# Norm factors from transposes, bursts moved off instruction borders, and a few reordered splits in a retention and HGRN2 step

## The chip, the cores and the metric

The kernel runs on one core of one Trainium2 chip. Its time is the device time of one execution in microseconds (us). Five engines run side by side, each with its own instruction stream: TensorE (PE in the profile; PEld are its weight loads), VectorE (DVE), ScalarE (ACT), GpSimd (POOL) and SyncE (SP), which issues most transfers.

## The reference

One layer of a decoder step. The input is normalised, projected to eight groups of 512 columns, and two kinds of heads run on them: four retention heads (rotary, fixed decay) and four HGRN2 heads (a forget gate per element). Both are normalised per head, gated, concatenated and projected back. 2048 prompt tokens run from a zero state, and 8 single tokens from given states.

```python
def rmsnorm(x, g):
    return x * lax.rsqrt(jnp.mean(x * x, axis=-1, keepdims=True) + NORM_EPS) * g

def mixer_layer(x, pos, s_ret, s_hg, norm_g, w_in, ret_g, hg_g, lb, w_out):   # cut
    h = rmsnorm(x, norm_g)
    p = (h @ w_in).astype(jnp.float32)            # 1024 -> 8 x 512
    rq, rk, rv, rg, hq, hf, hi, hgate = jnp.split(p, 8, axis=-1)
    rq, rk = rotary(rq, pos), rotary(rk, pos) * RET_DK ** -0.5
    o_ret, s_ret_new = chunked_decay_recurrence(rq, rk, rv, log_gamma, s_ret)
    o_ret = head_rmsnorm(o_ret, ret_g) * jax.nn.silu(rg)
    logf = jnp.logaddexp(jnp.log(lb), jnp.log1p(-lb) + jax.nn.log_sigmoid(hf))
    kin = (1.0 - lb) * jax.nn.sigmoid(-hf)
    o_hg, s_hg_new = chunked_decay_recurrence(jax.nn.silu(hq), kin, hi, logf, s_hg)
    o_hg = head_rmsnorm(o_hg, hg_g) * jax.nn.silu(hgate)
    return x + jnp.concatenate([o_ret, o_hg], -1) @ w_out, s_ret_new, s_hg_new
```

The outputs are the final-normalised results of prompt and sample and the four new states.

## The kernel before

**Products in three parts.** Every large fp32 product is made of three: each operand is split into a high and a low part (`hi_lo`: ACT rounds, DVE subtracts), and `three` runs high x high, high x low, low x high in a reduced fp32 form in which a matmul is one record of the profile. A plain fp32 matmul is two records; a transpose is one. Each record has a weight load beside it.

**Stage 1, the token pairs (to about 580 us).** The tokens are 8 pairs of 256. For each pair and each of three sets of weight columns, a seven-product scheme (`CHAIN`: operands `A..`, `S1` to `S4` of the tokens, `B..`, `T1` to `T4` of the weights) gives the projections for values, gates, queries and keys in banks `pv<pair><a to d>`. `v_pair(i, after)` writes one pair in program order; the lists `after[n]` say what is emitted behind product n of it: loads, splits, sums of the next weights, and the small matmuls `pgd` for the sample tokens (`wg_decode`, whose weights `wgr` are loaded by `wg_load` and stored as `ws..T` sums by `wg_spool`). The first set normalises the tokens: `rs_all` holds the factor of each token in a column, one per 128 tokens, computed on POOL. A product needs it along the free axis in every partition. `spread_dg` makes diagonal matrices on DVE (identity times factor), and `spread` multiplies a matrix of ones with them (`prs`, 128 x 128, two per pair), copies the bank to `rb` on DVE, and `tok_ops` multiplies the raw tokens by it. `decode_dg` and `decode_spread` (`dgd`, `prsd`) do the same for the 8 sample tokens. In the second and third set of weight columns the sums of the weights come from DRAM through loads `T1l` to `T4l`.

**Stage 2, the HGRN heads (about 580 to 885 us).** The loop runs over `order`, pairs of a half of the tokens and a head. `hgrn_proj` writes the projections of the next head (`pjfh`, `pjqh`, line 1039), which read the x split made by `x_steps` in four parts (`xh`, `xl`). The current head's recurrence (`hgrn_rec`) works on 1024 tokens in levels of 1, 2, 4, ... 64: `levels2(1)` and `levels2(3)` each write a burst of 64 tiny fp32 matmuls (`small`; `plh`, 32 columns of weights, 16 moving columns): 128 records, and with their weight loads 256 instructions; `scores0` (`pah`) and `scores3` are shorter. `merge` interleaves the filling work with the recurrence: `levels` is a list of (fraction, step), and a step is emitted as soon as that share of the filling work has been emitted. This text order is TensorE's order. In the last unit the filling work is the first rows of the output projection (`py`, line 1670), which read the output weights (`woh`, `wol`, made by `wo1`: loads `wor`, four splits, of which two make `wol` on DVE) and the retained outputs (`o_load`, `o_split`: `or` to `oc_h`, `oc_l`).

**Stage 3 (from about 885 us)** is the rest of the output projection, again with seven products.

**What sets the order.** TensorE and POOL keep the order of the program text. DVE, ACT and SP are ordered by a scheduler within the dependencies; `behind(f)` holds what `f` emits behind the latest instruction of each of these three in the text, and `tc.issue_after` behind a given one. On each engine and transfer queue work runs in order.

Of the kernel before, what the change touches and what calls it, by code (L numbers as in the profile page):

```python
# [10 lines left out]
F32 = mybir.dt.float32  # L11
# [7 lines left out]
P = 128  # L19
# [4 lines left out]
NB = 8  # L24
# [17 lines left out]
def step_kernel(ctx, tc, a, out):  # L42
# [39 lines left out]
    wu = ps_tr.tile([P, P], F32, tag="tr", name="wu")  # L82
    for n in range(14):
        pe.matmul(wu, ones, ones, start=True, stop=True)

    zero = const.tile([P, 24], F32, name="zero")
    dve.memset(zero, 0.0)
# [16 lines left out]
    lmask = const.tile([P, len(SMALL) * 16], U8, name="lmask")  # L104
    rs_all = const.tile([P, T // P], F32, name="rs_all")
    rsd = const.tile([NB, 2], F32, name="rsd")
    const.tile([P, 168], F32, name="fill")
    dq, dk, df = (const.tile([P, 8, NB], F32, name=f"d{n}") for n in "qkf")

    def rsqrt_mean(dst, src, n, eps):  # L110
# [168 lines left out]

    spread_to = {}  # L280

    dgs = {}

    def spread_dg(i):
        t = vq.tile([P, GW], F32, tag="rk", name=f"dg{i}")
        dgs[i] = [t[:, :P], t[:, P : 2 * P]]
        for dg, c in zip(dgs[i], (2 * TOK[i], 2 * TOK[i] + 1)):
            dve.tensor_scalar(dg, ident, rs_all[:, c : c + 1], None, op0=ALU.mult)

    def spread(i):  # L290
        pt = ps_tr.tile([P, 2, P], F32, tag="tr", name=f"prs{i}")
        for j, dg in enumerate(dgs[i]):
            pe.matmul(pt[:, j], ones, dg, start=True, stop=True)
        dst = vq.tile([P, GW], F32, tag="rq", name=f"rb{i}")[:, :256]
        dve.tensor_copy(dst, pt.rearrange("p a b -> p (a b)"))
        spread_to[i] = dst

    sop, lows = {}, {}

    def past(i, f):  # L300
        if i not in lows:
            return f()
        with tc.issue_after(lows[i]):
            f()

    def tok_ops(i, held=None):
        store = held.append if held is not None else lambda f: f()
        r0, r1 = xr[i]
        for j, r in enumerate((r0, r1)):
            if not spooled(i):  # L310
                for k in range(4):
                    kk = 4 * j + k
                    dve.scalar_tensor_tensor(  # L313
                        r[:, k], r[:, k], g_in[:, kk : kk + 1], spread_to[i], op0=ALU.mult, op1=ALU.mult
                    )
            kk = slice(4 * j, 4 * j + 4)
            bb = (slice(3 * slot(i), 3 * slot(i) + 1), slice(3 * slot(i) + 1, 3 * slot(i) + 3))[j]
            ra = r.rearrange("p k (o t) -> p o k t", t=P)[:, : 1 + j]
            hi_lo(ablk[0][:, bb], ablk[1][:, bb], ra)
            if not spooled(i):  # L320
                store(lambda kk=kk, r=r: sp.dma_start(a_dram[TOK[i]][:, kk], r))
        if spooled(i):
            return
        lows[i] = next(x for x in reversed(nc.cur_bb.bb.instructions) if x.engine == dve.engine)
        a11, a21, a12, a22 = r0[:, :, :P], r0[:, :, P:], r1[:, :, :P], r1[:, :, P:]
        ta, tb = (rawp.tile([P, 2, 4, P], F32, tag="raw", name=f"S{n}_{i}") for n in range(2))
        s2, s3, s1, s4 = ta[:, 0], ta[:, 1], tb[:, 0], tb[:, 1]
        dve.tensor_tensor(s1, a21, a22, op=ALU.add)
        dve.tensor_tensor(s2, s1, a11, op=ALU.subtract)
        dve.tensor_tensor(s3, a11, a21, op=ALU.subtract)  # L330
        dve.tensor_tensor(s4, a12, s2, op=ALU.subtract)
        sraw[i] = (ta, tb)
        for n, t in enumerate(sraw[i]):
            store(lambda n=n, t=t: sp.dma_start(s_dram[TOK[i]][n], t))
# [280 lines left out]
            dve.tensor_scalar(t, t, rsd[:, ty : ty + 1], None, op0=ALU.mult)  # L615
            sp.dma_start(vd_dram[ty], t)

    dgd = sm.tile([NB, NB], F32, tag="dgd", name="dgd", bufs=1)

    def decode_dg():  # L620
        dve.tensor_scalar(dgd, ident[:NB, :NB], rsd[:, 1:2], None, op0=ALU.mult)

    def decode_spread():
        pt = ps_tr.tile([P, NB], F32, tag="tr", name="prsd")
        pe.matmul(pt, ones[:NB, :], dgd, start=True, stop=True)
        rb = sm.tile([P, NB], F32, tag="rbd", name="rbd", bufs=1)
        act.activation(rb, pt, AF.Copy)
        dve.tensor_tensor(xs, xs, rb.unsqueeze(1).to_broadcast([P, KT, NB]), op=ALU.mult)
# [61 lines left out]
    tok_load(2)  # L690
    wv_comb(2)
    wv_comb(3)
    spread_dg(2)
    for ty in (1, 0):
        for c in range(2):
            ps = bank([P, GW], f"pv1{c}{ty}")
# [221 lines left out]
    for i in range(2, n_tok):  # L918
# [13 lines left out]
        if same(i + 1):  # L932
            for op in ("S1", "S2", "S3", "S4"):
                sop[i + 1, op] = sop[i, op]
        elif i + 1 < n_tok:
            if not spooled(i + 1):
                after[0] += [lambda i=i: past(i, lambda: spread_dg(i + 1))]
                after[1] += [lambda i=i: spread(i + 1)]
            tied = behind if i >= N_V - 1 else lambda f: f()
            late = 2 if same(i) else 0  # L940
            after[2 + late] += [
                lambda i=i, t=tied: t(lambda: tok_ops(i + 1)), lambda i=i, t=tied: t(lambda: s_split(i + 1, 0))
            ]
            after[4 + late // 2] += [lambda i=i, t=tied: t(lambda: s_split(i + 1, 1))]
# [11 lines left out]
            after[4] += [lambda i=i: rot_load(i + 1)]  # L956
        if i == 2:
            after[3] += [lambda: behind(decode_values_out)]
            after[0] += [decode_dg]
            after[2] += [decode_spread]  # L960
        if m < 3:
            if 2 <= j < 6:
                after[0] += [lambda m=m, k=j - 2: wg_load(m, k)]
                after[4] += [lambda m=m, k=j - 2: wg_decode(m, k), lambda m=m, k=j - 2: wg_spool(m, k)]
            if j == 7:
                after[0] += [lambda m=m: wg_decode_out(m)]
                for n, (_, op, _) in enumerate(CHAIN):
                    after[n] = [lambda m=m, op=op: wg_fetch(m, op)] + after[n]
        if i >= N_V - 1 and j in (7, 0) and i < n_tok - 1:
# [211 lines left out]
    def keep_state(half, hd, name):  # L1181
# [3 lines left out]
        dve.tensor_copy(old, pools["S"][hd - NH])  # L1185
        return old

    def hgrn_rec(half, h, u):
        name = f"h{half}{h}"
        hd = NH + h  # L1190
# [142 lines left out]
        def then_decode(n, f):  # L1333
            return joined(f, *(lambda hd=hd: behind(lambda: d_mm(hd)) for hd in mm_at.get((half, h, n), ())))

        levels = [(0.0, products), (0.07, scores0), (0.32, then_decode(1, lambda: levels2(1))), (0.4, lambda: behind(load)),
                  (0.58, then_decode(3, lambda: levels2(3))), (0.84, scores3),
                  (0.95, t["k0"]), (0.98, t["k1"])]
        rest = [(0.02, begin), (0.13, t["u0"]), (0.28, t["u1"]), (0.43, t["o0"]), (0.47, t["o1"]),
                (0.53, t["n0"]), (0.59, t["n1"]), (0.65, t["t0"]), (0.73, t["t1"]), (0.73, last)]  # L1340
# [144 lines left out]
    def unit(i):  # L1485
# [3 lines left out]
        if i in SEG_MAJOR:  # L1489
            for n in range(len(SEGS[half])):  # L1490
                group = []
                for sub in subs:
                    group += sub[n]
                if (i, n) in sides:
                    group = weave(group, sides[i, n](), 0.0, 1.0 if i not in (3, 7) or (i, n) == (3, 1) else 0.6)
                steps += group
        else:
            for sub in subs:
# [59 lines left out]
    def o_split(c):  # L1558
# [1 line left out]

    x2 = x_steps(2)
    wo0, wo1 = wo_steps(0), wo_steps(1)
    side_at += [(7.3, lambda: o_load(0)), (7.48, lambda: o_split(0)), (7.8, lambda: o_load(1)),
                (7.7, wo1[1][0]), (7.85, wo1[1][1])]
    sides = {
        (3, 1): lambda: x2[:3],
# [286 lines left out]
    for c in range(PLAIN):  # L1853
        fill += out_steps(c)
    fill = place(fill, sorted([
        *((0.02 + 0.04 * n, lambda s=s: behind(s)) for n, s in enumerate(wo1[2])),
        (0.03, wo1[1][2]), (0.07, wo1[1][3]),
        (0.2, d_norm), (0.6, t2_load), (0.65, lambda: op_load(p0)), (0.75, lambda: op_s12(p0)),
        (0.8, lambda: op_s34(p0)), (0.85, lambda: op_a(p0)), (0.9, lambda: op_s23(p0)),
# [132 lines left out]
```

## Time and profile before

| | |
|---|---|
| time, median of 3 runs | 1035.85 us (1034.95 to 1038.08) |
| profiled execution, its own time | 1041.4 us |
| its span | 1039.6 us |
| granted TensorE clock, mean | 0.997 |
| TensorE busy | 1020.8 us, 98% of the span, 8359 records |
| DVE, ACT, POOL busy | 747.7, 559.5, 129.1 us |
| transfers | 255.63 MB, 246 GB/s on average |

A row of the timeline gives the start, the duration, the engine, the line and the operands; `x62` is a run of 62 alike, and a bracket gives the idle time before the row and what ended it. Successive matmuls overlap, so what a matmul costs is the distance from its start to the next start, not its duration. In the table of waits "issue" is idle time for which no awaited event is recorded. A row of windows gives the stretch, then for each engine the busy time and the number of records, then the granted clock, the mean busy share of the DMA engines and GB/s.

### The profile page before, as it was taken

What the parts mean: (1) busy time and instruction counts of PE and PEld (TensorE: products, weight loads), DVE (VectorE), ACT (ScalarE), POOL (GpSimd) and SP (SyncE); (2) the same over time, 40 slices, a digit from 0 to 9 for tenths busy, and PEclk for the clock granted to TensorE, in tenths of its full rate; (3) what the DMA queues carried; (4) which work ended last, traced back from release to release, by engine and by line L of the source; (5) the groups of instructions that cost most, each with busy time, mean ns of one, the idle gap of its engine ahead of it and who ended that gap; (6) DMA issues with size and microseconds to landing.
All of it is one profiled execution on the core that took longest, in us unless ns stands there. A gap on an engine that the chain in (4) does not pass through costs nothing.

```text
span 1039.6 us, 21590 instructions
## 1 busy us (share of the span) xinstructions
PE 1020.8 (98%) x8359; PEld 845.4 (81%) x8359; DVE 747.7 (72%) x1387; ACT 559.5 (54%) x1233; POOL 129.1 (12%) x231
## 2 busy tenths in 40 slices
PE   9999999999999999999999999999999999999997
PEld 7777778787778888878888889898788877888775
DVE  6886676787666876666666777869758676668886
ACT  7853345635435765545554766666556465543242
POOL 0410001000000111111111200111012102311122
PEclk9999999999999999999999999999999999999999
DMA  8699999679998975486776686845954495575652
GB/s 294 219 326 337 331 325 327 255 249 325 307 341 292 373 240 164 163 259 219 241 245 175 231 330 222 271 141 187 291 168 138 119 374 197 165 283 203 234 174 102
DMA packets 151271, 255.63 MB, mean 246 GB/s; under 512 B 11424, under 2 KB 79280, under 8 KB 151040
## 3 DMA queue, kind: packets, MB, share of 16 engines
q1 hardware_dynamic: 141408, 225.03, 64.2%
q0 software_dynamic: 7440, 24.76, 6.2%
q10 hardware_dynamic: 2320, 4.46, 1.1%
q8 instruction: 66, 1.08, 0.4%
q14 instruction: 37, 0.30, 0.1%
HBM read 166.51 MB, written 87.69 MB: 245 GB/s over the span
## 4 chain that ended last, share of the span: by engine, by line
PE 77%; DMA 12%; DVE 5%; ACT 3%; issue 2%; SPq 1%; POOL 0%; POOLq 0%; ACTq 0%; DVEq 0%
PE po L360 11%; PE pjfh L1039 8%; PE pjqh L1039 7%; PE py L1670 4%; DMA wgr<-in_w 2%; PE plh L1255 2%; PE pur L751 1%; PE por L757 1%; DMA T3l<-ws1T 1%; PE poh L1142 1%; DMA xn<-in_x_prompt 1%; DMA or<-o_dram 1%; PE por L759 1%; PE par L744 1%; PE puh L1126 1%
## 5 line engine op out<-in xcount | busy, mean ns | idle before, releaser
L1235 ACT ACTIVATE kepth<-kh 128x1024 f32<-128x1024 f32 x24 | 25.5, 1061 | 67.8 <-DVE kh L1225 67.8
L1039 PE MATMUL pjfh<-xh,w_h 128*128 128x512 f32 (+2 forms) x160 | 59.9, 374 | 0.8 <-ACT fxh L1087 0.8
L1039 PE MATMUL pjqh<-xh,w_h 128*128 128x512 f32 (+2 forms) x160 | 59.0, 369 | 0.0
L1039 PE MATMUL pjfh<-xh,w_l 128*128 128x512 f32 (+2 forms) x160 | 55.7, 348 | 2.2 <-issue 2.2
L1039 PE MATMUL pjfh<-xl,w_h 128*128 128x512 f32 (+2 forms) x160 | 55.8, 349 | 0.0
L1039 PE MATMUL pjqh<-xh,w_l 128*128 128x512 f32 (+2 forms) x160 | 55.7, 348 | 0.0
L1039 PE MATMUL pjqh<-xl,w_h 128*128 128x512 f32 (+2 forms) x160 | 55.6, 347 | 0.0
L1225 DVE TENSOR_TENSOR kh<-kh,fph 128x512 f32<-128x512 f32 x48 | 33.3, 694 | 18.0 <-PE plh L1255 12.2
L116 DVE TENSOR_TENSOR ab_l<-xr,ab_h 128x512 fp32r<-128x512 f32 (+1 forms) x40 | 37.5, 954 | 7.9 <-ACT ab_h L115 7.9
L782 DVE SCALAR_TENSOR_TENSOR obr<-por,omr,rg 128x128 f32<-128x128 f32 x64 | 18.0, 344 | 32.4 <-POOL omr L774 30.1
L772 ACT ACTIVATE obr<-por 128x128 f32<-128x128 f32 x64 | 16.9, 278 | 44.5 <-PE por L759 42.2
L115 ACT ACTIVATE ab_h<-xr 128x512 fp32r<-128x512 f32 (+1 forms) x40 | 32.4, 840 | 14.2 <-DVE xr L313 14.2
L1039 PEld LDWEIGHTS pjfh<-xh,w_l 128*128 128x128 f32 x160 | 30.2, 189 | 6.6 <-issue 2.6
L419 ACT ACTIVATE vo<-vo 128x512 f32<-128x512 f32 x32 | 20.1, 630 | 27.4 <-DVE vo L413 13.5
L1039 PEld LDWEIGHTS pjfh<-xh,w_h 128*128 128x128 f32 x160 | 30.3, 190 | 5.4 <-ACT fxh L1087 1.1
L1039 PEld LDWEIGHTS pjqh<-xh,w_h 128*128 128x128 f32 x160 | 30.4, 190 | 4.8 <-issue 1.2
L1039 PEld LDWEIGHTS pjqh<-xh,w_l 128*128 128x128 f32 x160 | 30.1, 188 | 4.0
L1228 DVE TENSOR_TENSOR qqh<-qqh,fph 128x512 f32<-128x512 f32 x48 | 32.8, 683 | 0.0
L1039 PEld LDWEIGHTS pjfh<-xl,w_h 128*128 128x128 f32 x160 | 30.3, 190 | 2.7
L1039 PEld LDWEIGHTS pjqh<-xl,w_h 128*128 128x128 f32 x160 | 30.2, 189 | 2.9
L313 DVE SCALAR_TENSOR_TENSOR xr<-xr,g_in,rb 128x256 f32<-128x256 f32 x64 | 27.2, 480 | 7.2 <-issue 4.6
L1670 PE MATMUL py<-wol,oc_h 128*128 128x512 f32 x64 | 25.2, 394 | 2.9 <-issue 2.1
(1840 smaller groups left out, 3379.2 us busy)
## 6 DMA issues: line engine op xcount, KB each, us to landing
xr<-a_dram SPq DMA_DIRECT2D x24, 512.0 KB, 5.3
S<-s_dram SPq DMA_DIRECT2D x24, 512.0 KB, 5.5
xn<-in_x_prompt SPq DMA_DIRECT2D x32, 256.0 KB, 3.4
xr<-in_x_t SPq DMA_DIRECT2D x16, 512.0 KB, 6.1
a_dram<-xr SPq DMA_DIRECT2D x16, 512.0 KB, 4.0
s_dram<-S SPq DMA_DIRECT2D x16, 512.0 KB
wgr<-in_w SPq DMA_DIRECT2D x16, 512.0 KB, 7.9
xr<-a_dram SPq DMA_DIRECT2D x32, 256.0 KB, 4.1
```

What stands on the lines that cost most here:

```text
L115: act.activation(h, src, AF.Copy)
L116: dve.tensor_tensor(l, src, h.bitcast(F32), op=ALU.subtract)
L313: dve.scalar_tensor_tensor(r[:, k], r[:, k], g_in[:, kk : kk + 1], spread_to[i], op0=ALU.mult, op1=ALU.mult)
L360: pe.matmul(ps, xx, ww, start=(first and n == 0), stop=(last and n == 2), skip_group_check=more)
L419: act.activation(o, src, AF.Silu)
L782: dve.scalar_tensor_tensor(o[:, cc], po[:, h], ms[:, h : h + 1], rb_of[c, "g"][:, cc], op0=ALU.mult, op1=ALU.mult)
L1039: pe.matmul(ps, ww[:, kk], x[:, k, b0 : b0 + n], start=(k == 0 and i == 0), stop=(k == KT - 1 and i == 2),)
L1225: dve.tensor_tensor(kv[:, :, 0, :], kv[:, :, 0, :], two[:, :, 1:2].to_broadcast([P, nb, b]), op=ALU.mult)
L1228: dve.tensor_tensor(qv[:, :, 1, :], qv[:, :, 1, :], two[:, :, 0:1].to_broadcast([P, nb, b]), op=ALU.mult)
L1235: act.activation(ss[:, 512:], k[:, :HALF], AF.Copy)
L1255: pe.matmul(dst[32 * i : 32 * i + 32, c], kk, qq, start=True, stop=True)
L1670: pe.matmul(ps, o[:, kk], w[:, k % 4, i * 512 : (i + 1) * 512], start=(k == 0 and n == 0), stop=(k == KT - 1 and n == 2),)
```

## The change

1. **Transposes for the factors.** `spread_dg`, `decode_dg` and `past` are gone. `spread` transposes a column of `rs_all` that is repeated 128 times by its access pattern, and `decode_spread` does the same with a column of `rsd`. A transpose of a matrix whose columns are all alike has the factors along the free axis in every partition, which is what the product of ones with the diagonal matrix gave. The unused tile `fill` grows by the 8 elements of the tile `dgd`, so the tiles behind it stay where they were.
2. **Warm-up.** Sixteen 32 x 16 matmuls follow the fourteen of 128 x 128 at the start; their result is read by nobody.
3. **Bursts.** `MOVE`, keyed by half of the tokens, head and level, shifts four of the fractions at which `levels2` is emitted.
4. **Reordered.** `wg_decode` and `wg_spool` of the first set come behind product 5, not 4; `wg_decode_out` is held `behind`; in unit 7 the weaving of side steps into the projection ends at 0.6 of it, in unit 3 it always runs to the end; the second `o_load` comes before the weight loads; the four splits `wo1` come at 0, 0, 0.04 and 0.08 of the filling work instead of 0.02, 0.06, 0.1 and 0.14.

```diff
     for n in range(14):
         pe.matmul(wu, ones, ones, start=True, stop=True)
+    for n in range(16):
+        pe.matmul(wu[:32, :16], ones[:, :32], ones[:, :16], start=True, stop=True)
...
-    const.tile([P, 168], F32, name="fill")
+    const.tile([P, 176], F32, name="fill")
...
-    def spread_dg(i):
-        t = vq.tile([P, GW], F32, tag="rk", name=f"dg{i}")
-        dgs[i] = [t[:, :P], t[:, P : 2 * P]]
-        for dg, c in zip(dgs[i], (2 * TOK[i], 2 * TOK[i] + 1)):
-            dve.tensor_scalar(dg, ident, rs_all[:, c : c + 1], None, op0=ALU.mult)
-
     def spread(i):
         pt = ps_tr.tile([P, 2, P], F32, tag="tr", name=f"prs{i}")
-        for j, dg in enumerate(dgs[i]):
-            pe.matmul(pt[:, j], ones, dg, start=True, stop=True)
+        for j in range(2):
+            c = 2 * TOK[i] + j
+            pe.transpose(pt[:, j], rs_all[:, c : c + 1].to_broadcast([P, P]), ident)
...
     def decode_spread():
         pt = ps_tr.tile([P, NB], F32, tag="tr", name="prsd")
-        pe.matmul(pt, ones[:NB, :], dgd, start=True, stop=True)
+        pe.transpose(pt, rsd[:, 1:2].to_broadcast([NB, P]), ident[:NB, :NB])
...
             if not spooled(i + 1):
-                after[0] += [lambda i=i: past(i, lambda: spread_dg(i + 1))]
                 after[1] += [lambda i=i: spread(i + 1)]
...
-                after[4] += [lambda m=m, k=j - 2: wg_decode(m, k), lambda m=m, k=j - 2: wg_spool(m, k)]
+                after[6 - m] += [lambda m=m, k=j - 2: wg_decode(m, k), lambda m=m, k=j - 2: wg_spool(m, k)]
             if j == 7:
-                after[0] += [lambda m=m: wg_decode_out(m)]
+                after[0] += [lambda m=m: behind(lambda: wg_decode_out(m))]
...
+    MOVE = {(0, 0, 1): 0.065, (1, 0, 1): 0.065, (1, 1, 3): -0.065, (1, 3, 1): 0.055}
...
-        levels = [(0.0, products), (0.07, scores0), (0.32, then_decode(1, lambda: levels2(1))), (0.4, lambda: behind(load)),
-                  (0.58, then_decode(3, lambda: levels2(3))), (0.84, scores3),
+        levels = [(0.0, products), (0.07, scores0), (0.32 + MOVE.get((half, h, 1), 0), then_decode(1, lambda: levels2(1))), (0.4, lambda: behind(load)),
+                  (0.58 + MOVE.get((half, h, 3), 0), then_decode(3, lambda: levels2(3))), (0.84, scores3),
...
-                    group = weave(group, sides[i, n](), 0.0, 1.0 if i not in (3, 7) or (i, n) == (3, 1) else 0.6)
+                    group = weave(group, sides[i, n](), 0.0, 1.0 if i < 7 else 0.6)
...
-    side_at += [(7.3, lambda: o_load(0)), (7.48, lambda: o_split(0)), (7.8, lambda: o_load(1)),
+    side_at += [(7.3, lambda: o_load(0)), (7.48, lambda: o_split(0)), (7.46, lambda: o_load(1)),
...
-        *((0.02 + 0.04 * n, lambda s=s: behind(s)) for n, s in enumerate(wo1[2])),
+        *((0.04 * max(n - 1, 0), lambda s=s: behind(s)) for n, s in enumerate(wo1[2])),
```

What this makes of the orders is shown at three places. The numbers at the ends of tile names count tiles and differ between the two programs; so do the line numbers, by 18 to 20 here, since lines are gone above.

TensorE in stage 2, the second half of the tokens, at 748 us of the profile before: `pjfh` is the projection of the next head, `plh` the burst, `poh` the output of the head before. Before:

```order
L1039 MATMUL pjfh_512_8102<-xh_7480,w_l 128x512
L1255 MATMUL plh_8125<-kepth_8057 32x16 x32
L1255 MATMUL plh_8125<-qqh_7582,kh_7581 32x16 x32
L1039 MATMUL pjfh_512_8102<-xh_7480,w_h 128x512
L1039 MATMUL pjfh_512_8102<-xl_7481,w_h 128x512
L1039 MATMUL pjfh_512_8102<-xh_7480,w_l 128x512
L1039 MATMUL pjfh_512_8102<-xh_7480,w_h 128x512
L1039 MATMUL pjfh_512_8102<-xl_7481,w_h 128x512
L1039 MATMUL pjfh_512_8102<-xh_7480,w_l 128x512
L1142 MATMUL poh_8214<-v_7705,Ah 128x128 x2
```

and now:

```order
L1019 MATMUL pjfh_512_8092<-xh_7470,w_h 128x512
L1019 MATMUL pjfh_512_8092<-xl_7471,w_h 128x512
L1019 MATMUL pjfh_512_8092<-xh_7470,w_l 128x512
L1019 MATMUL pjfh_512_8092<-xh_7470,w_h 128x512
L1019 MATMUL pjfh_512_8092<-xl_7471,w_h 128x512
L1019 MATMUL pjfh_512_8092<-xh_7470,w_l 128x512
L1237 MATMUL plh_8122<-kepth_8047 32x16 x32
L1237 MATMUL plh_8122<-qqh_7572,kh_7571 32x16 x32
L1122 MATMUL poh_8204<-v_7695,Ah 128x128 x2
```

The burst stands six products later, right ahead of `poh`.

DVE in the first rows of the output projection (855 us): `dech` ends the chain of products of forget gates, `kh` and `qqh` are the updates of the current head, `sth` is its state. Before:

```order
L1542 TENSOR_TENSOR wol_9552<-wor_9453,woh_9551 128x1024
L1216 TENSOR_TENSOR fph_9553<-fph_9553 128x16
L1216 TENSOR_TENSOR fph_9553<-fph_9553 128x8
L1218 COPY dech_9561<-fph_9553 128x8
L1225 TENSOR_TENSOR kh_9123<-kh_9123,fh_9122 128x512
L1228 TENSOR_TENSOR qqh_9124<-qqh_9124,fh_9122 128x512
L1275 TENSOR_TENSOR Abh_9583<-pah_9584,pk 128x256
L1261 COPY_PREDICATED Abh_9583<-lmask,pah_9584 128x128
L1225 TENSOR_TENSOR kh_9123<-kh_9123,fph_9553 128x256x2
L1228 TENSOR_TENSOR qqh_9124<-qqh_9124,fph_9553 128x256x2
L1134 SCALAR_TENSOR_TENSOR sth_9636<-oldh_9571,dech_9036,puh_9637 128x128
L1542 TENSOR_TENSOR wol_9552<-wor_9513,woh_9551 128x1024
```

and now:

```order
L1198 TENSOR_TENSOR fph_9543<-fph_9543 128x8
L1200 COPY dech_9551<-fph_9543 128x8
L1524 TENSOR_TENSOR wol_9542<-wor_9435,woh_9541 128x1024
L1524 TENSOR_TENSOR wol_9542<-wor_9503,woh_9541 128x1024
L1207 TENSOR_TENSOR kh_9113<-kh_9113,fh_9112 128x512
L1210 TENSOR_TENSOR qqh_9114<-qqh_9114,fh_9112 128x512
L1257 TENSOR_TENSOR Abh_9575<-pah_9576,pk 128x256
L1243 COPY_PREDICATED Abh_9575<-lmask,pah_9576 128x128
L1207 TENSOR_TENSOR kh_9113<-kh_9113,fph_9543 128x256x2
L1210 TENSOR_TENSOR qqh_9114<-qqh_9114,fph_9543 128x256x2
L1114 SCALAR_TENSOR_TENSOR sth_9628<-oldh_9565,dech_9026,puh_9629 128x128
L1114 SCALAR_TENSOR_TENSOR sth_9628<-sth_9628,dech_9026,puh_9629 128x128 x3
```

Both `wol` splits come right behind `dech`; before, the first stood among the products of forget gates and the second behind `sth`.

ACT at 700 us: `xh` is the high part of the x split, `fsh` and `fxh` the sigmoids that read the bank `pjfh`, `Ah` and `kh` belong to the head before and the next. Before:

```order
L1319 ACTIVATE Ah<-Abh_6919 32x8x32 x3
L115 ACTIVATE xh_7166<-xr_7343 128x1024
L1086 ACTIVATE fsh_7419<-pjfh_768_7346 128x264
L1087 ACTIVATE fxh_7418<-pjfh_768_7346 128x264
L1088 ACTIVATE fh_6990<-fsh_7419,lb,lb_168 128x264
L1089 ACTIVATE kh_6991<-fxh_7418,lb_168 128x264
```

and now:

```order
L1301 ACTIVATE Ah<-Abh_6909 32x8x32 x3
L1066 ACTIVATE fsh_7407<-pjfh_768_7336 128x264
L1067 ACTIVATE fxh_7406<-pjfh_768_7336 128x264
L1068 ACTIVATE fh_6980<-fsh_7407,lb,lb_184 128x264
L1069 ACTIVATE kh_6981<-fxh_7406,lb_184 128x264
L117 ACTIVATE xh_7156<-xr_7333 128x1024
```

The split stands behind the four operations that read the bank.

More of the change, by code (lines that the diff above doesn't have):

```diff
@@ L280, in step_kernel @@
     spread_to = {}
-    dgs = {}
-    def spread_dg(i):
-        t = vq.tile([P, GW], F32, tag="rk", name=f"dg{i}")
-        dgs[i] = [t[:, :P], t[:, P : 2 * P]]
-        for dg, c in zip(dgs[i], (2 * TOK[i], 2 * TOK[i] + 1)):
-            dve.tensor_scalar(dg, ident, rs_all[:, c : c + 1], None, op0=ALU.mult)
     def spread(i):
         pt = ps_tr.tile([P, 2, P], F32, tag="tr", name=f"prs{i}")
-        for j, dg in enumerate(dgs[i]):
-            pe.matmul(pt[:, j], ones, dg, start=True, stop=True)
+        for j in range(2):
+            c = 2 * TOK[i] + j
+            pe.transpose(pt[:, j], rs_all[:, c : c + 1].to_broadcast([P, P]), ident)
         dst = vq.tile([P, GW], F32, tag="rq", name=f"rb{i}")[:, :256]
@@ L296, in spread @@
         spread_to[i] = dst
[L298 to L304, printed above, removed]
+    sop = {}
     def tok_ops(i, held=None):
@@ L323, in tok_ops @@
             return
-        lows[i] = next(x for x in reversed(nc.cur_bb.bb.instructions) if x.engine == dve.engine)
         a11, a21, a12, a22 = r0[:, :, :P], r0[:, :, P:], r1[:, :, :P], r1[:, :, P:]
@@ L616, in decode_values_out @@
             sp.dma_start(vd_dram[ty], t)
-    dgd = sm.tile([NB, NB], F32, tag="dgd", name="dgd", bufs=1)
-    def decode_dg():
-        dve.tensor_scalar(dgd, ident[:NB, :NB], rsd[:, 1:2], None, op0=ALU.mult)
     def decode_spread():
         pt = ps_tr.tile([P, NB], F32, tag="tr", name="prsd")
-        pe.matmul(pt, ones[:NB, :], dgd, start=True, stop=True)
+        pe.transpose(pt, rsd[:, 1:2].to_broadcast([NB, P]), ident[:NB, :NB])
         rb = sm.tile([P, NB], F32, tag="rbd", name="rbd", bufs=1)
@@ L692, in step_kernel @@
     wv_comb(3)
-    spread_dg(2)
     for ty in (1, 0):
@@ L958, in step_kernel @@
             after[3] += [lambda: behind(decode_values_out)]
-            after[0] += [decode_dg]
             after[2] += [decode_spread]
```

## The prediction

> **What bounds the kernel now.** I read the profile's page first, then TensorE's waits, then the timeline at the longest of them.
>
> ```profile
> span 1039.6 us, 21590 instructions
> PE 1020.8 (98%) x8359; PEld 845.4 (81%) x8359; DVE 747.7 (72%) x1387; ACT 559.5 (54%) x1233; POOL 129.1 (12%) x231
> q8 instruction: 66, 1.08, 0.4%
> PE 77%; DMA 12%; DVE 5%; ACT 3%; issue 2%; SPq 1%; POOL 0%; POOLq 0%; ACTq 0%; DVEq 0%
> ```
>
> TensorE is busy 98% of the span; the rest is 18.8 us. So an edit is worth what it takes out of TensorE's own work or out of its waits; DVE's 72% and ACT's 54% count only where TensorE stands still for them. Of TensorE's waits, those that the change touches, or that could be next (total, times, longest):
>
> ```profile
> PE pjfh L1039 <- issue: 2.2, 1, 2.2
> PE py L1670 <- issue: 2.1, 1, 2.1
> PE pjfh L1039 <- ACT fxh L1087: 0.8, 1, 0.8
> PE py L1670 <- DVE wol L1542: 0.8, 1, 0.8
> PE pv8a L360 <- ACT s L400: 0.6, 1, 0.6
> PE pah L1273 <- DVE fph L1216: 0.2, 1, 0.2
> ```
>
> The two longest are "issue": no operand is late. The timeline shows both right behind a burst of 128 small `plh` records (columns: start, duration, instruction, idle time before it):
>
> ```profile
> 748.02 0.70 PE L1255 MATMUL plh<-kepth 128*32 128x16 f32 x62
> ...
> 749.22 0.50 PE L1039 MATMUL pjfh<-xh,w_h 128*128 128x512 f32 x1
> ...
> 750.02 0.40 PE L1039 MATMUL pjfh<-xh,w_h 128*128 128x512 f32 x1
> 750.25 0.39 PE L1039 MATMUL pjfh<-xl,w_h 128*128 128x512 f32 x1
> 752.80 0.50 PE L1039 MATMUL pjfh<-xh,w_l 128*128 128x512 f32 x1 [2.16 <-issue]
> ...
> 860.51 0.51 PE L1670 MATMUL py<-woh,oc_h 128*128 128x512 f32 x1
> 863.12 0.50 PE L1670 MATMUL py<-wol,oc_h 128*128 128x512 f32 x1 [2.11 <-issue]
> ```
>
> The neighbours step by 0.23 us (750.02 to 750.25), so the stalls cost 2.55 - 0.23 = 2.32 and 2.61 - 0.23 = 2.38 us. Are they at borders of instruction blocks? Each record is two instructions (weights and matmul). Between the two stalls lie
>
> ```profile
> 752.75:863.05 110.30, 107.22 (x1658) 87.28 (x1658) 76.14 (x160) 62.44 (x146) 17.81 (x31) 0.98 0.63 207
> 742.84:750.48 7.64, 7.64 (x162) 6.21 (x160) 7.06 (x14) 3.08 (x6) 0.00 (x0) 1.00 1.02 305
> 852.38:860.74 8.36, 7.60 (x162) 6.08 (x160) 6.80 (x16) 5.20 (x7) 0.00 (x0) 1.00 1.05 331
> 788.00:846.00 58.00, 57.93 (x875) 47.00 (x865) 38.44 (x82) 34.28 (x87) 12.03 (x21) 1.00 0.54 183
> ```
>
> 1658 + 1658 recorded instructions (first row), and the program has 12 more of other kinds there: 3328 = 13 x 256. The queue of kind "instruction" moved 1.08 MB in 66 packets, 16 KB each, which is one packet per 256 of TensorE's some 16,840 instructions. And one such packet lies in each of the stretches 750.45 to 751.45 and 860.80 to 861.85, while TensorE stands still:
>
> ```profile
> q8 instruction: 1, 0.02, 5.5%
> q8 instruction: 1, 0.02, 5.7%
> ```
>
> Set against the program's count, no packet of the trace starts before TensorE is 64 instructions short of the border ahead of the block it will need; from there it has 320 instructions to arrive. The second and third rows above are these 320 (160 records) for the two stalls: 7.64 and 8.36 us, with the DMA engines full (share 1.02, 1.05), since a burst spends 256 instructions in about 1.2 us (748.02 to 749.22). TensorE went on 9.96 and 10.74 us after the start of the rows (752.80 - 742.84, 863.12 - 852.38). Elsewhere 320 instructions last longer or the DMA engines are emptier (fourth row: 0.54) and nothing shows. [...]
>
> **The bursts.** `MOVE` puts one burst six products later at 748 and one at 860, one six earlier (797.7), and one twelve later (611). All later instructions also shift by +29 (16 added warm-up matmuls x 4 = +64; eight spreads -4 each; the decode one -2; another -1). Counted in the built programs, the two bursts began 10 and 2 instructions ahead of a border and begin 225 and 217 ahead of one now; the nearest other 256-instruction burst begins 38 ahead. At 748 the 320 instructions were 23 products, eight `puh` records and the burst: 7.64 = 23 x 0.23 + 1.2 + 1.15 for `puh` and the changes of shape. Now they are 30 products, sixteen `puh` records and 225/256 of the burst: 6.9 + 1.05 + 1.9 (between 1.15 and twice that) = 9.85 us, against 9.96 needed. At 860 it is the same list but for a few instructions (and the wait for `wol` in that stretch is gone, below): 9.9, against 10.74. Left over at before's latencies: 0.1 + 0.85 = 0.95. Gained: 2.32 + 2.38 - 0.95 = **3.7 us**. Bounds: 0 (it returns at other borders) and 4.7. No operand of a moved burst is late: the one moved earlier, by 1.4 us, reads `qqh` of
>
> ```profile
> 790.64 0.68 DVE L1228 TENSOR_TENSOR qqh<-qqh,fph 128x512 f32<-128x512 f32 x1
> 228.36 0.61 PE L293 MATMUL prs<-dg,ones 128*128 128x128 f32 x4
> 228.72 0.47 PE L360 MATMUL pv10a<-T2h,s100h 128*128 128x512 f32 x1
> 229.03 0.39 PE L360 MATMUL pv10a<-T2l,s100h 128*128 128x512 f32 x1
> 700.16 0.60 PE L1118 MATMUL pkh<-ident,kh 128*128 128x128 f32 x4
> 62.77 0.61 PE L293 MATMUL prs<-dg,ones 128*128 128x128 f32 x4
> 63.48 0.50 PE L360 MATMUL pv2a<-T2h,s20h 128*128 128x512 f32 x1
> ```
>
> which ended at 791.32, 6.4 us ahead of it.
>
> **The spreads.** The same rows price these. From 228.36 to 229.03 pass 0.67 us, one product of 0.23 and the spread: 0.44 us for four records, 0.11 each, an fp32 matmul being two. A transpose is one record, and four `pkh` transposes last as long (0.60) as four `prs` records (0.61). So 0.22 us are saved per spread. The one at 62.77 saves nothing: the next product starts 0.71 behind it, not 0.36, so it waits for something else. 7 x 0.22 = 1.55, and about 0.15 for the decode spread: **1.7 us**. That a column is read 128 times shows in no row; if a transpose cost both records' time the gain is 0, and 2.0 is the most. DVE's 17 multiplies by the identity go too; they are off the path, so they count nothing; what they waited for (the factors) TensorE now waits for, no later than before.
>
> **Splits and load.**
>
> ```profile
> 699.80 1.06 ACT L115 ACTIVATE xh<-xr 128x1024 fp32r<-128x1024 f32 x1
> 855.13 1.23 DVE L1542 TENSOR_TENSOR wol<-wor,woh 128x1024 fp32r<-128x1024 f32 x1
> L1540 ACT ACTIVATE woh<-wor x4: 1039/1048/1072, 848.6 to 855.9; 128x1024 fp32r<-128x1024 f32 x4
> L1535 SPq DMA_DIRECT2D wor<-in_w_out x4: 440/852/5127, 833.6 to 841.1; - x4
> 72.09 0.39 PE L360 MATMUL pv2a<-T3h,s20l 128*128 128x512 f32 x1
> 73.39 0.50 PE L360 MATMUL pv2c<-B22h,s21h 128*128 128x512 f32 x1
> 92.86 0.39 PE L360 MATMUL pv3a<-T3h,s30l 128*128 128x512 f32 x1
> 94.47 0.50 PE L360 MATMUL pv3c<-B22h,s31h 128*128 128x512 f32 x1
> ```
>
> The fourth x split (699.80, 1.06 us) stood ahead of the two ACT operations (`fsh`, `fxh`) whose end frees TensorE's bank, for which TensorE waited 0.8. Behind them it holds up nobody there: **0.8**. Its own reader is a whole projection part away. The second `wol` now precedes `kh` and `qqh` on DVE, so it is done before TensorE asks: **0.8**, and 0.2 for `pah`, ahead of which the first `wol` stood. Next late there are the parts of `woh`, the last of which starts on ACT at 855.9; with them the gain could be half, so bounds 0.4 and 1.0. On SP the second `or` load goes ahead of eight weight loads, so `wor`, issued up to 841.1, comes later by one transfer; the first use is at 848.6 and the last at 855.9, and that cover hides it. Were it gone, the 5 us of the longest such issue would be TensorE's.
>
> **Four `pgd` groups** of the first set move twelve products (2.8 us) later. The second of them takes 94.47 - 92.86 = 1.61 us in the rows above, the first, whose weights are there, 73.39 - 72.09 = 1.30. Two of the four are late, by about 0.3 each: **0.6**.
>
> **What it adds.** The 16 small warm-up matmuls (32 records) come ahead of the first product:
>
> ```profile
> 7.21 0.50 PE L360 MATMUL pv<-wv_h,ab_h 128*128 128x512 f32 x1 [0.46 <-ACT wv_h L115]
> 185.12 1.06 ACT L115 ACTIVATE T1h<-T1l 128x1024 fp32r<-128x1024 f32 x1 [1.40 <-DMA T1l<-ws1T]
> ```
>
> They fill the idle 0.46 us. Small records cost from 0.01 us (a burst's 1.2/128) to 0.11: 0.3 to 3.5 us; they have 16 columns like a burst's, so I take the low end, 0.3 and hidden, and **+0.2** for the chance of more. At 185 ACT waits for loads of stored sums and TensorE for ACT; on SP one weight load and stores pass to other places there, which may make these late by part of a load: **+0.3**, bounds 0 and 1.5.
>
> **Sum** for the profiled execution: -3.7 - 1.7 - 0.8 - 1.0 - 0.6 + 0.2 + 0.3 = -7.3 us, 1041.4 to 1034.1. The profiled execution is 5.5 us above the median (1035.85) of runs of 1034.95 to 1038.08; if part of that is transfers made slower, the unprofiled stalls are shorter. I take -6.4 on the median: **1029.5 us**.
>
> **Rivals.** (1) Only the stalls go, and the small waits are followed at once by the next in line (`woh`, the loads at 185): -3.7 - 1.7 + 0.5 for what is added = -4.9, 1031.0. For it: DVE is 72% busy and only reordered; against: the spreads are TensorE's own time. (2) The stalls are not cured: the cause is the slow packet (it lies past the ends of rows of 7.64 and 8.36 us), and with every border shifted by 29 another crossing under full DMA, or the burst now 38 ahead of a border, loses them. The rest alone: 1.7 + 1.8 + 0.6 - 0.5 = 3.6, less half of the 1.8, 2.7: 1033.2. For it: at 860 my balance is already negative by 0.85; against: the other bursts near a border lie where DMA is emptier. (3) Slower: the loads around 185. The chain of waits has 12% DMA, and ACT waits 1.40 for `T1l` there; four such loads, T1 to T4, feed the products of that pair. A weight load moved behind the sums' stores and run against them makes them later; from 7.3 us of lateness in all, about 1.8 for each, it eats everything, and at 3.5 each the time is 1036 + 6.7 = 1042.5. Against: the queue that loads them is not touched, only its neighbour.
>
> **Chances.** Forecast 0.55 (1027 to 1031.5), rival 1 0.2, rival 2 0.19, rival 3 0.06. 0.3% is 3.1 us, about what a measurement of this kernel tells from no change, so "faster" is below 1032.7: 0.53 + 0.17 + 0.05 = 0.75; the same 0.20; slower 0.05. Range 1026.0 (stalls wholly gone, every term at its bound: -9.7) to 1033.6 (rival 2).
>
> **What will show it.** Right: no "issue" wait over 0.3 us behind a `plh` burst at about 745 and 855; `prs` x16 not x32, its group at 0.22 us; no wait on `fxh` or `wol`; first product still at 7.2. Wrong: an issue wait at another border (rival 2); `woh` or `wor` among the waits (rival 1); the wait of `pv8a` on `s` well over 0.6 us (rival 3). If the stalls go and the time does not fall by 3 us, the stall was the profiler's own, or something fills its place.

## The result, and the profile after

The changed kernel takes 1041.28 us (median of 22 runs, 1038.5 to 1044.31), the kernel before 1036.98 (22 runs, 1034.81 to 1042.78). The ratio is 1.0036, with a 95% interval of 1.0024 to 1.0048: some 3.7 us slower, where 6.4 us faster were forecast. The profiled executions show the same span for both, 1039.6 and 1039.5 us; the one of before was among its slowest runs (1041.4), the one of the change in the middle of its own (1041.33).

The head of the page of the changed kernel:

```profile
span 1039.5 us, 21608 instructions
PE 1019.5 (98%) x8374; PEld 844.1 (81%) x8374; DVE 744.8 (72%) x1370; ACT 557.5 (54%) x1233; POOL 125.0 (12%) x231
```

TensorE is busy 1.3 us less, in spite of 15 records more. What the forecast counted as removed is gone from TensorE's waits, and others stand in its place (waits of the changed kernel: total, times, longest):

```profile
PE pd L588 <- DVE obh L1137: 4.3, 1, 4.3
PE prs L288 <- POOL rs_all L114: 1.7, 3, 0.6
PE pv2a L348 <- ACT ab_h L117: 1.6, 1, 1.6
PE pv8c L348 <- DVE B22l L118: 1.3, 1, 1.3
PE poth L1144 <- DVE obh L1137: 0.8, 2, 0.6
PE pah L1255 <- DVE dq L1329: 0.5, 1, 0.5
```

There is no issue wait left, none on `fxh`, none on `wol`. The largest new one, 4.3 us, has a tail. The timeline of the changed kernel behind it, and its windows (busy time, then the granted clock, DMA share and GB/s):

```profile
798.45 1.08 PE L588 MATMUL pd<-dS,dqp 128*32 128x256 f32 x8 [4.28 <-DVE obh L1137]
799.46 0.80 PE L1019 MATMUL pjqh<-xh,w_h 128*128 128x512 f32 x1
800.06 0.63 PE L1019 MATMUL pjqh<-xl,w_h 128*128 128x512 f32 x1
800.48 0.63 PE L1019 MATMUL pjqh<-xh,w_l 128*128 128x512 f32 x1
...
803.17 0.40 PE L1019 MATMUL pjqh<-xh,w_h 128*128 128x512 f32 x1
803.40 0.39 PE L1019 MATMUL pjqh<-xl,w_h 128*128 128x512 f32 x1
```

```profile
796.00:800.00 4.00, 1.55 (x9) 0.50 0.01 4
800.00:804.00 4.00, 4.00 (x14) 0.65 0.02 6
804.00:808.00 4.00, 4.00 (x24) 1.00 1.07 314
```

After the wait TensorE runs at half its clock for some 4 us (0.50 from 798.45 to 802.80): the products step by 0.42 us (800.06 to 800.48), later by 0.23 again. Half the clock for that long costs about 2 us on top of the wait. The whole cost shows between two landmarks, an output of a head before the place and the transposes behind it. Before:

```profile
757.69 0.38 PE L1142 MATMUL poh<-v,Ah 128*128 128x128 f32 x2
800.89 0.38 PE L1164 MATMUL poth<-ident,obh 128*128 128x128 f32 x2
```

and after:

```profile
754.22 0.38 PE L1122 MATMUL poh<-v,Ah 128*128 128x128 f32 x2
803.86 0.38 PE L1144 MATMUL poth<-ident,obh 128*128 128x128 f32 x2
```

The changed kernel arrives 3.5 us ahead and leaves 3.0 us behind: 6.4 us lost in one place. Ahead of the first issue stall the changed kernel was 0.6 us behind (`puh` at 742.63 and 742.04), so it gained about 4.1 us there; that stall had such a tail too in the profiled execution of before:

```profile
752.00:756.00 4.00, 3.20 (x16) 0.67 0.62 166
756.00:760.00 4.00, 4.00 (x26) 0.91 0.29 49
```

One term can be read directly, a spread in the timeline of the changed kernel: from 230.25 to 230.70 pass 0.45 us, one product of 0.23 and 0.22 for the two transposes, where it was 0.44. The repeated column adds nothing to the price worked out in the forecast.

```profile
230.25 0.38 PE L288 MATMUL prs<-ident,rs_all 128*128 128x128 f32 x2
230.38 0.48 PE L348 MATMUL pv10a<-T2h,s100h 128*128 128x512 f32 x1
230.70 0.40 PE L348 MATMUL pv10a<-T2l,s100h 128*128 128x512 f32 x1
```

### The profile page after: what moved, and what is told of

Same layout as the page of the kernel before. It is cut to its first block, busy times and chain, and to the rows that moved or that the text cites. A ratio compares the mean times of both kernels' runs of the same rounds, so it can differ in the third digit from the quotient of the medians.

```text
span 1039.5 us, 21608 instructions
## 1 busy us (share of the span) xinstructions
PE 1019.5 (98%) x8374; PEld 844.1 (81%) x8374; DVE 744.8 (72%) x1370; ACT 557.5 (54%) x1233; POOL 125.0 (12%) x231
## 4 chain that ended last, share of the span: by engine, by line
PE 84%; DMA 7%; ACT 3%; DVE 2%; issue 1%; POOL 1%; SPq 0%; POOLq 0%; ACTq 0%; DVEq 0%
PE po L348 11%; PE pjqh L1019 8%; PE pjfh L1019 8%; PE py L1652 3%; PE plh L1237 2%; DMA v_dram<-vo 1%; PE par L726 1%; PE pur L733 1%; PE puh L1106 1%; PE por L739 1%; DMA xn<-in_x_prompt 1%; PE por L741 1%; PE pv2a L348 1%; PE poh L1122 1%; PE poh L1124 1%
## 5 line engine op out<-in xcount | busy, mean ns | idle before, releaser
L1652 PE MATMUL py<-woh,oc_h 128*128 128x512 f32 x64 | 26.7, 417 | 0.0
```

Of the source, the lines that this page charges most:

```text
L1652: pe.matmul(ps, o[:, kk], w[:, k % 4, i * 512 : (i + 1) * 512], start=(k == 0 and n == 0), stop=(k == KT - 1 and n == 2),)
```

## Experiments

The ratios are to runs of the kernel before on the same chip, with 95% intervals.

### The issue stalls: fetches of instruction blocks?

**A second profile of before**, no edit.

> The kernel before, unchanged, for a second profile. If the two issue stalls at instruction borders belong to every execution: both again, 2.2 and 2.1 us at 750 and 860, and a reduced clock behind the first. If they depend on how the fetch meets the other transfers: one or both gone and the profiled span some 4 us shorter (1035). Time: the same as before, ratio 1.000.

Ratio 1.0004 (0.9983 to 1.0024), profiled span 1036.8 us. The stalls are at the same places but shorter, and a third shows at another burst (785.55). No reduced clock follows. Its waits:

```profile
PE plh L1255 <- issue: 1.1, 1, 1.1
PE py L1670 <- issue: 1.0, 1, 1.0
PE pjfh L1039 <- issue: 0.7, 1, 0.7
```

So the 2.2 and 2.1 us on which the forecast rested were one execution's; this one shows 2.8 in all, without a tail. A third profile without a shift (that of "That move alone", below, whose edit lies elsewhere) has 1.8 and 2.1 at the two places. Full transfers alone do not account for the size: in the 20 us from 740 the DMA engines were less busy in the first profile, with 2.16 us of stall (share 0.80, and 1.03 from 742.30 to 750.45), than in the second, with 0.73 (0.98), and in the 20 us from 780, around the third stall, they were busy 0.38.

**Only the two bursts moved.**

```diff
+    MOVE = {(1, 0, 1): 0.065, (1, 3, 1): 0.055}
```

> Before, with only the two bursts moved that preceded the stalls (half 1, heads 0 and 3, level 1). Theory (the stalls are in every execution): no issue wait over 0.3 us, about 4.1 us gained at 750 (stall 2.3 and the reduced clock behind it) and 2.4 at 860, together -6.5: ratio 0.994. Rival (the stalls were in the one profiled execution alone, or are taken over at once by the next wait): no issue wait, but the time within 2 us of before, ratio 0.998 to 1.001.

Ratio 0.9998 (0.9979 to 1.0018): nothing gained. Without the shift of 29 instructions the bursts, six products later, begin 254 and 246 ahead of a border, so the border falls inside the burst. At the first place the stall went with it (timeline):

```profile
748.40 0.70 PE L1257 MATMUL plh<-kepth 128*32 128x16 f32 x62
...
748.97 0.68 PE L1257 MATMUL plh<-qqh,kh 128*32 128x16 f32 x61
752.21 0.20 PE L1257 MATMUL plh<-qqh,kh 128*32 128x16 f32 x1 [2.55 <-issue]
752.34 0.71 PE L1142 MATMUL poh<-v,Ah 128*128 128x128 f32 x4
```

TensorE ran 127 of the 128 records, 254 instructions, and stood 2.55 us ahead of the last. No operand tells that record from its neighbour; the border does. Ahead of this stall and of those at 750 in the two profiles of before lie the same 5681 matmul records, though it was a product that stood there then and is the end of a burst now. At the second place the wait falls ahead of record 7340 in all three, and is 0.27 us here. Both expectations missed: at the first place the wait was not removed, and the time did not fall although the second all but went.

**Only a shift**, before with 28 more instructions at the start.

```diff
+    for n in range(7):
+        pe.matmul(wu[:32, :16], ones[:, :32], ones[:, :16], start=True, stop=True)
```

> The kernel before with seven small matmuls (28 instructions) added at the start and nothing else: the two bursts that began 10 and 2 instructions ahead of a border begin 238 and 230 ahead of one. Theory (the stalls are fetches of instruction blocks): no issue wait of TensorE over 0.3 us, and the time falls by what the two profiles of before show there, 2.8 us (1.0, 0.7 and 1.1) to 6.1 us (2.2, 2.1 and 1.8 of reduced clock): ratio 0.994 to 0.997. Rival (they have another cause): waits of 0.7 to 2.2 us at the same two places, ratio 1.000.

The two stalls are gone. One issue wait is left in its waits, of 0.5 us, at 795.80, behind the burst that now begins 27 instructions ahead of a border:

```profile
PE pjqh L1041 <- issue: 0.5, 1, 0.5
```

Ratio 0.9982 (0.9965 to 0.9999): 1.9 us, below the 2.8 to 6.1 expected, whose low end lies inside the interval. Where the instructions lie is thus shown to be the cause of the stalls, and removing them to be worth about half of what the one profile promised. Seven of the profiles, with those of before, have issue waits of 0.2 us or more, thirteen together. The ten in the four profiles without instructions added at the start stand at three places, ahead of which lie 5681, 6189 and 7339 records; in the built programs the borders there are 1024 and 2304 instructions apart, 4 x 256 and 9 x 256. The other three (0.5, 0.5 and 0.2 us) are on `pjqh`. Most borders pass without a wait: a run has some 65 (16,844 instructions in before), and none of these profiles has more than three such waits. What sets the size of a stall, from 0.2 to 2.55 us, stays open.

### The burst that was moved earlier

**That move alone** on the kernel before.

```diff
+    MOVE = {(1, 1, 3): -0.065}
```

> Before, with only the burst of half 1, head 1, level 3 moved six products earlier. Theory (pd follows that burst, needs the bank that obh empties, and obh now stands on VectorE behind the five operations of the burst): a wait of pd on obh of 4 to 4.5 us near 798 and 2.6 us of reduced clock behind it, +7 us, ratio 1.007. Rival (in the changed kernel TensorE only gave back its lead there, since obh comes at a fixed time): a wait under 1 us and no measurable difference, ratio 1.000 to 1.002.

The wait is there to the tenth in its waits, and half the clock behind it in its windows:

```profile
PE pd L600 <- DVE obh L1157: 4.3, 1, 4.3
```

```profile
796.00:800.00 4.00, 1.23 (x9) 0.65 0.01 2
800.00:804.00 4.00, 4.00 (x10) 0.50 0.02 5
```

Ratio 1.0044 (1.0021 to 1.0068), 4.6 us: the theory's mechanism, less than its 7 us (the profiled execution, 1047.56 us, was the slowest of its twelve). The rival (a lead given back) falls, since this kernel had no lead: its issue stall at 750, 1.8 us, was still there.

**The changed kernel without it.**

```diff
-    MOVE = {(0, 0, 1): 0.065, (1, 0, 1): 0.065, (1, 1, 3): -0.065, (1, 3, 1): 0.055}
+    MOVE = {(0, 0, 1): 0.065, (1, 0, 1): 0.065, (1, 3, 1): 0.055}
```

> The changed kernel without that one move (the burst then begins 26 instructions ahead of a border). Theory: the wait of pd on obh and the reduced clock behind it are gone, -7 us against the changed kernel: about 1034, ratio to before 0.997. Rival (the lead is given back at the next wait): the wait only shrinks or moves, 1039 to 1041, ratio 1.002 to 1.004. If the border at 26 instructions counts, an issue wait of 1 to 2 us near 800.

Ratio 0.9972 (0.9951 to 0.9993), 1035.69 us, and neither the wait nor an issue wait: as the theory had it, 0.0064 or 6.6 us below the changed kernel. The lower clock is not one profile's either: the mean granted clock of the changed kernel's 22 executions is 0.993 to 0.997 (median 0.995), that of the twelve without the move 0.994 to 0.999 (median 0.998). One key of a table turned a gain into a loss.

**Why is `obh` late?** The timeline of VectorE before,

```profile
795.03 1.13 DVE L1157 SCALAR_TENSOR_TENSOR obh<-poh,orsh,v 128x128 f32<-128x128 f32 x4 [2.42 <-POOL orsh L112]
```

and in the changed kernel, with the operation of POOL that makes `orsh` for it:

```profile
790.47 1.04 POOL L114 TENSOR_TENSOR orsh<-orsh,mhalf 128x4 f32<-128x4 f32 x1
794.23 0.72 DVE L1207 TENSOR_TENSOR kh<-kh,fph 128x512 f32<-128x512 f32 x1 [5.10 <-PE plh L1237]
794.87 0.68 DVE L1210 TENSOR_TENSOR qqh<-qqh,fph 128x512 f32<-128x512 f32 x1
795.47 0.61 DVE L1243 COPY_PREDICATED Abh<-lmask,plh 128x128 f32<-128x128 uint8 x2
796.06 0.69 DVE L1207 TENSOR_TENSOR kh<-kh,fph 128x512 f32<-128x512 f32 x1
796.67 0.68 DVE L1210 TENSOR_TENSOR qqh<-qqh,fph 128x512 f32<-128x512 f32 x1
797.27 1.12 DVE L1137 SCALAR_TENSOR_TENSOR obh<-poh,orsh,v 128x128 f32<-128x128 f32 x4
```

Two things moved with the burst. In the text, `then_decode(3, ...)` hangs the sample tokens' product `pd` on it, so `pd` came six products earlier as well; it takes one of the two buffers of `ps_o` (line 866 of the changed kernel), which `obh` must empty first (`poh`, line 1118). And the scheduler put the six operations that follow the burst (two of them one row, `x2`) ahead of `obh`. Before, `obh` ran as soon as `orsh` was there. Now `orsh` was there at 791.51, but VectorE stood idle for 5.10 us until the burst had run, with `obh` behind `kh` in its order, and `obh` began 5.8 us late, at 797.27, and ended at 798.39. To tell the two apart, the burst stays early and `pd` goes back:

```diff
-                  (0.58 + MOVE.get((half, h, 3), 0), then_decode(3, lambda: levels2(3))), (0.84, scores3),
+                  *(((0.58 + MOVE[half, h, 3], lambda: levels2(3)), (0.58, then_decode(3, lambda: None)))
+                    if (half, h, 3) in MOVE else ((0.58, then_decode(3, lambda: levels2(3))),)), (0.84, scores3),
```

> The changed kernel, with the burst of half 1, head 1, level 3 six products earlier as there, but pd left at its old place behind those products. Theory (pd needs the bank that obh empties, and on VectorE obh stands behind the five operations of the burst): obh ends as late as before, so a wait of about 3 us (4.3 - 1.4) remains near 798, with some reduced clock: 1038 to 1040, ratio 1.001 to 1.003. Rival (only pd's place in TensorE's order matters): the wait is gone, as in the kernel without the move: 1035.7, ratio 0.997.

```profile
PE pd L588 <- DVE obh L1137: 2.7, 1, 2.7
```

In its waits 2.7 us remain (above), and the ratio is 1.0019 (1.0003 to 1.0034). So the place of `pd` is 1.6 of the 4.3 us; the rest stays as long as the burst is early, with `obh` behind its followers. An early burst with `obh` ahead of its followers was not run.

### The factors

**`pgd` back behind product 4**, without the bad move.

```diff
...
-                after[6 - m] += [lambda m=m, k=j - 2: wg_decode(m, k), ...
+                after[4] += [lambda m=m, k=j - 2: wg_decode(m, k), ...
...
```

> The changed kernel without the move of that burst, and with the pgd groups of the first set back behind product 4. Theory (the later place of pgd put three squares of x behind the copy s of the product's bank on ScalarE, so the norm factors came late): the three waits of prs on rs_all (0.58 each, 2.2 us with the change of shape) are gone, and 0.6 us of waits on wgr are back: 1.6 us below the kernel without the move, 1034.1, ratio 0.9957. Rival (the waits of prs come from the transposes): they stay, ratio 0.997.

The waits of `prs` are gone from its table of waits, those on `wgr` back:

```profile
PE pgd L588 <- DMA wgr<-in_w: 2.1, 3, 1.1
```

The cause stands on ACT. With `pgd` later, in the timeline of the changed kernel `s`, which must wait for a product of the next pair, stands ahead of the squares of x from which the factors are made:

```profile
104.06 0.60 ACT L388 ACTIVATE s<-pv4a 128x512 f32<-128x512 f32 x1 [2.18 <-PE pv4a L348]
104.56 0.62 ACT L269 ACTIVATE xn<-xn 128x512 f32<-128x512 f32 x1
...
107.26 0.43 PE L288 MATMUL prs<-ident,rs_all 128*128 128x128 f32 x2 [0.58 <-POOL rs_all L114]
```

Before, these squares ran from 101.01 to 102.36, ahead of `s`. The mechanism is shown; in time the two waits trade, since 2.1 us of waits on `wgr` came back and not 0.6: ratio 0.9978 (0.9962 to 0.9995), against 0.9972 with the later `pgd`, not the 0.9957 expected.

**The old spreads** in the changed kernel without the bad move: diagonals and the product of ones, and 8 small matmuls fewer at the start for the same borders.

```diff
...
-            pe.transpose(pt[:, j], rs_all[:, c : c + 1].to_broadcast([P, P]), ident)
+            pe.matmul(pt[:, j], ones, dg, start=True, stop=True)
...
```

> The changed kernel without the move of that burst, and with the diagonal matrices and the product of ones in place of the transposes (and eight small matmuls fewer at the start, so that borders lie within 2 instructions of where they were). Theory (a transpose costs half of it, and does not cause the waits): waits on the factors stay, now by way of the diagonal, and 1.7 us more: about 1037.4, ratio 0.9988. Rival (the transposes cause the waits): no wait at prs, and the same or less time, ratio 0.996 to 0.997.

```profile
PE prs L295 <- DVE dg L290: 3.2, 3, 1.1
```

The waits stay and grow (its waits, above), from 1.7 to 3.2 us, since the diagonal stands between factor and TensorE. Ratio 1.0001 (0.999 to 1.0013) against 0.9972: the transposes did not cause the waits. The difference, 0.0029 or 3.0 us, is the 1.7 us of TensorE's own time that were expected and the 1.5 us by which these waits are longer, as near as intervals that just overlap can tell.

### The splits, and the best kernel

**No burst moved, `pgd` behind product 4**, the shift by 28 left (the line is compared with the kernel with `pgd` back, above).

```diff
-    MOVE = {(0, 0, 1): 0.065, (1, 0, 1): 0.065, (1, 3, 1): 0.055}
+    MOVE = {}
```

> The changed kernel with no burst moved at all, and with the pgd groups behind product 4. The shift by 28 instructions alone leaves the two bursts 238 and 230 ahead of a border. Theory (the shift does it; the remaining moves only make operations on VectorE late): no issue wait over 0.5 us, and the wait of poth on obh near 871 (1.6 us with the move of the burst there) is gone or under 0.6: ratio 0.996 to 0.997. Rival (the moves are needed as well): issue waits of 1 to 2 us are back near 750 or 860, ratio 0.9985 to 1.0.

Ratio 0.9949 (0.9929 to 0.9969), 1032.82 us, no issue wait at all: better than both kernels, by more than expected. `poth` still waits 0.8 on `obh` near 871, half of what it waited with the move there and more than the 0.6 expected. The same kernel once more, on another chip:

> The same kernel as the best so far (no burst moved, pgd behind product 4), beside the next one on one chip: 0.994 to 0.997 again if the gain is real, 0.998 or more if it was the luck of one session.

Ratio 0.9971 (0.9949 to 0.9994), 1034.55 us: a gain again, of 3 rather than 5 us.

**The four reorderings undone**, once with the three other moves and once without any:

```diff
...
-                    group = weave(group, sides[i, n](), 0.0, 1.0 if i < 7 else 0.6)
+                    group = weave(group, sides[i, n](), 0.0, 1.0 if i not in (3, 7) or (i, n) == (3, 1) else 0.6)
...
-                (7.46, lambda: o_load(1)),
+                (7.8, lambda: o_load(1)),
...
-        *((0.04 * max(n - 1, 0), lambda s=s: behind(s)) for n, s in enumerate(wo1[2])),
+        *((0.02 + 0.04 * n, lambda s=s: behind(s)) for n, s in enumerate(wo1[2])),
```

> The changed kernel without the move of the burst of head 1, with pgd behind product 4, and with the four reorderings of stage 2 undone (x split, output weight splits, load of the retained outputs). Theory (they are worth their waits): the waits on fxh and wol, 0.8 us each, and 0.2 to 0.5 more at pah are back, and the time is 1.8 us above the same kernel with them: ratio 0.9995. Rival (what they free is lost at the next wait): the same ratio as with them, 0.9978.

> The same with the four reorderings of stage 2 undone: what is left of the change is then the transposes, the shift by 28 instructions and the held decode copies. If what the reorderings free is given back at the next wait (pah behind fxh, poth behind wol), the ratio is that of the kernel beside it within 0.001; if they are worth their waits, it is 0.0018 higher.

The waits on `fxh` and `wol` come back as they were, here in the first of the two kernels,

```profile
PE pjfh L1019 <- ACT fxh L1067: 0.9, 1, 0.9
PE py L1652 <- DVE wol L1524: 0.8, 1, 0.8
```

and the time does not rise: 0.9965 (0.9946 to 0.9984) with the moves, where the kernel with the reorderings had 0.9978 on another chip, and 0.9955 (0.9931 to 0.9979) without, beside 0.9971 on the same chip. Neither pair shows the 1.8 us, and with their intervals each leaves room for less than that. With the reorderings (and the three moves), TensorE's timeline has waits a little further on:

```profile
702.84 0.43 PE L1255 MATMUL pah<-qqh,kh 128*32 128x64 f32 x16 [0.54 <-DVE fph L1198]
870.72 1.11 PE L1144 MATMUL poth<-ident,obh 128*128 128x128 f32 x4 [1.57 <-DVE obh L1137]
```

What `fxh` and `wol` free is given back at `pah` and at `poth`: with the reorderings undone `pah` has no such wait and `poth` waits 0.2. The wait of `poth` shrinks without the move of the burst there (0.76), so it is in part that move's. Behind it stands VectorE, which in the same kernel waits for a transfer of results and then runs the burst's six followers ahead of `obh`:

```profile
866.68 0.69 DVE L1696 TENSOR_TENSOR oS<-or 128x512 f32<-128x512 f32 x1 [4.44 <-DMA out_y_prompt<-yc]
...
870.32 1.12 DVE L1137 SCALAR_TENSOR_TENSOR obh<-poh,orsh,v 128x128 f32<-128x128 f32 x4
```

So TensorE that comes earlier there only waits longer. In one profile with the reorderings, that of the changed kernel without the early burst, `py` itself still waited 0.8 us near 853, for the transfer of a part of `wol`.

## Why the prediction was wrong

**The step that failed** is in "The bursts": "No operand of a moved burst is late: the one moved earlier, by 1.4 us, reads `qqh` of" a row that ended 6.4 us ahead. That was so, and was not the question. A product hung on the same step and came along, and the burst's followers on VectorE changed places with the operation that frees the bank. The orders of TensorE and VectorE in the built program showed both, and only the row that writes the burst's operand was looked at there. The forecast priced that one move at nothing; the runs price it at 0.0044 to 0.0064 of the time, 4.6 to 6.6 us, and this alone turns a gain into a loss. Without it the change gains 2.9 us (0.9972), still less than half of the 6.4 forecast; the rest lies in the terms below. The slower rival (loads at 185) was the wrong place: `pv8a` no longer waits there, `pv8c` now waits 1.3 for `B22l`, and 1.1 became 1.3 us.

**The stalls**: the mechanism was right as far as the borders of 256 instructions go, and rival 2 falls for the changed kernel, which has no issue wait. That a fetch is late only under full transfers was not shown, and around the third stall the DMA share was 0.38 (780 to 800). The size was not right. The term was 3.7 us; the shift alone measures 1.9 us (0.1 to 3.6). One profile, of an execution 4.4 us above the later median of 1036.98, was taken for all; the forecast had said that the stalls of other executions may be shorter, and took 0.9 us off the sum where half of the term was due. The tail of reduced clock behind the first stall was missed in the rows that were quoted: the clock column there read 0.98 for the stretch from 752.75 to 863.05. The residual of 0.95 us did not appear either.

**The transposes**: 0.22 us per spread, as worked out. That TensorE waits for the factors "no later than before" failed, 1.7 us in three waits, but the edit to blame is the one counted as a gain of 0.6: `pgd` moved later took ACT's order with it. In time the two cancel.

**Splits**: both waits went, 1.6 us, and the next in line took them. This was rival 1, but its next in line was misjudged: not `woh`, but `pah` and `poth`.

**Warm-up**: the first product starts at 7.25 us, not 7.21: free, as taken.

## What to carry to other kernels

Before moving a step earlier in a fixed order, list what is emitted with it and what the scheduled engines then place ahead of the operations that free banks, and compare those engines' orders at that place. An engine that keeps its order holds up everything behind an operation whose operand comes late (VectorE stood idle for 5.10 us ahead of `kh` here, with `orsh` for the `obh` behind it there from 791.51 on); a step's own operands are the smaller half. A stall in one profiled execution is a size only for that one (2.2 and 2.1 us here, and 0.7 and 1.0 in the next): profile the unchanged kernel twice before pricing it. Removing a short wait gains nothing if the same chain waits again a few us on (here 0.54 us at `pah` behind the 0.8 us freed at `fxh`): look for that next wait before counting the first.

## What the runs showed of the hardware

**Half the clock came with idles of TensorE.** Behind an idle of 4.28 us (the changed kernel), of 2.69 us (with `pd` back) and of 2.16 us (the first stall in the first profile of before) the granted clock fell to 0.50, 0.74 and 0.67 in a window of 4 us, and behind 1.63 us (the wait on `ab_h` at 57.65 of the changed kernel, whose windows follow) to 0.74:

```profile
56.00:60.00 4.00, 2.37 (x8) 0.84 0.70 217
60.00:64.00 4.00, 4.00 (x15) 0.74 1.00 361
```

Behind the second stall in the first profile of before (2.11 us) the granted clock stayed at 1.00 (863.10 to 867.00), so the length of the idle alone does not decide it. Apart from the end of each run, the profiles of before and of the changed kernel have three stretches of half clock: 753.35 to 756.76 of before, begun 0.55 us behind the end of its idle, and of the changed kernel 58.70 to 62.11, begun 1.05 us behind, and 795.98 to 802.80, begun 1.8 us within the idle of 4.28. They last 3.4, 3.4 and 6.8 us. What tells the idle of 2.16 us from that of 2.11 is not shown.

**A border stalled TensorE in the middle of a burst**: 2.55 us between two records of one group that differ in nothing. Others did not: in the changed kernel the borders lie 225 and 217 instructions into the bursts of 748 and 860, and no issue wait is left.
